# A hybrid decoder layer on one core: diagonal masking moved from TensorE to GpSimd, some loads moved to the GpSimd queue, and the FFN's first weight pieces given an earlier place in memory

## The chip, the cores and the metric

The kernel runs on one core of one Trainium2 chip. The core has five engines that run their own instruction queues: TensorE (PE, with its weight loads shown as PEld), VectorE (DVE), ScalarE (ACT), GpSimd (POOL) and SyncE (SP), which here only issues DMA transfers. ACT issues some transfers too (ACTq in the trace). The metric is the device time of one launch in microseconds. The kernel before took 2703.38 us, the median of 3 runs (2702.57 to 2706.26).

## The reference

One decoder layer over 2048 positions of width 1024, in float32:

```python
a = rms_norm(h, pre_mix_g);  z = a @ w_in          # q | k | v | f | u_sg | v_sg
logits = q @ k.T / 8 + c[t] - c[s]                 # c = cumsum(log_sigmoid(f + f_bias)); 8 heads x 64
logits = where(s <= t, logits, -inf)               # causal
y_att = softmax(logits) @ v
y_sg = gelu(u) * (tril(w_s) @ layer_norm(gelu(v)) + b_s)
h += rms_norm(concat(rms_norm(y_att), rms_norm(y_sg)) @ w_out, post_mix_g)
h += rms_norm(relu(rms_norm(h) @ w_ff1)**2 @ w_ff2, post_ffn_g)
h += sigmoid(h @ w_g + b_g) * (p @ w_pe)
```

## The kernel before

Every large product is made of three TensorE products of rounded operands: a value is split into a piece `hi`, rounded to the type float32r, and the remainder `lo`, and `mm3` (lines 102 to 106) adds hi*hi, hi*lo and lo*hi into one PSUM bank. So each operand needs a rounding (an ACT cast, a DVE copy or a POOL `tensor_scalar`) and a subtraction (DVE, mostly).

The stages, in the order of time in the trace:

1. 0 to 566 us: the input projection in four blocks of 512 positions (`block`), with `maxima(b)` of the previous block mixed in. `maxima` computes, for each head and block, products of q and k (line 169) of which DVE takes row maxima (lines 172, 175); the row maxima later enter the attention's bias. It loads q and k from a DRAM scratch into two buffers each, `QM` and `KM`, by transfers that the ACT queue issues (lines 159 and 165). Each `KM` load serves four products.
2. 566 to about 1124 us: the attention. `steps` is a list of 320 steps (head, block of 512 queries, tile `j` of 128 keys), first the blocks 0 and 1 of all heads (96 steps), then block 2 (96 steps), then block 3 (128 steps). In program order `scores` runs `LA = 4` steps ahead of `weigh`. `scores` makes two products into a PSUM bank of a pool of two (`pS`, lines 644 and 647); in the four diagonal tiles of each (head, block) a third product adds a matrix with -1e30 above the diagonal (line 649: `dmask_r` times an identity `ident_r`). Because `MASKB` is 4 and `b < MASKB` always holds, the branch in which GpSimd masks (line 653) never runs. Then ACT takes the exponential (line 651), ACT or, for the tiles in `HI_DVE`, DVE rounds it (lines 659, 657), and DVE subtracts (line 660). `weigh` makes three products with V (lines 672 to 674). Mixed in by rates are the rest of `maxima(2)`, all of `maxima(3)` (its eight heads with four `KM` loads each fall between 556 and 880 us), the V projection of the last block (`late_v`) and, in blocks 2 and 3, the output projection `project` of earlier blocks.
3. About 1124 to 1190 us: the output projection of the last block (`last_proj`), with `prep_first` mixed in: it loads `h`, transposes it, writes `cS`, and makes the operands `B[m][0]` and `B[m][1]` of the FFN's first product. The FFN multiplies by a seven-product scheme over 2x2 blocks; `join` and `join_now` make the seven right operands (`m` = 1 to 7).
4. From 1190 us: FFN, first product, 32 units. `left(i)` makes the rounded pieces `w1p` of seven combinations of W1 tiles (sums in `ws`, line 1170; cast line 991, subtraction line 994; a ring of three tiles), two calls ahead of `ff1(i)`, which multiplies. Unit 0 alone runs in two passes of 42 matmuls: first `k` = 0, 1 for all seven `m`, then `k` = 2, 3, whose operands `join2` and `join3` finish meanwhile. After that the second product, the gate and the output, to 2700 us.

The program is written in a framework that orders each engine's queue at build time and inserts the waits; a tile of a pool that is opened over memory of earlier pools waits until those tiles are released. In the kernel before, `w1p` comes from a pool of its own, "w1pp" (line 1134), that is opened only after the pools of stages 2 and 3 have been closed (lines 1131 to 1133). The tiles `px` (line 964) hold the transposed pieces in `prep_first` (line 1092), the raw operands of `join2` (`jraw`, line 1125) and those of `prep_next` (line 1107), which prepares the second half of the positions during the FFN.

Of the kernel before, what the change touches and what calls it, by code (L numbers as in the profile page):

```python
# [9 lines left out]
F32 = mybir.dt.float32  # L10
F32R = mybir.dt.float32r
AF = mybir.ActivationFunctionType
ALU = mybir.AluOpType
# [4 lines left out]
P = 128  # L18
# [3 lines left out]
HD = 64  # L22
# [5 lines left out]
NB = S // TB  # L28
# [6 lines left out]
def trunk(ctx, tc, x, p, w_in, f_bias, sg_ln_g, sg_ln_b, sg_w, sg_b, att_out_g, sg_out_g,  # L35
# [4 lines left out]
    def pool(stack, name, bufs=1, space=None, side="left"):  # L40
        kw = {} if space is None else {"space": space}
        return stack.enter_context(tc.tile_pool(name=name, bufs=bufs, side=side, reuse_waits="tile", **kw))

    sc, ve, po, pe, sy = nc.scalar, nc.vector, nc.gpsimd, nc.tensor, nc.sync

    x, p, out = x[0], p[0, 0], out[0]
# [28 lines left out]
    ve.memset(dmask, 0.0)  # L75
    po.affine_select(out=dmask_r, in_=dmask, pattern=[[-1, P]], compare_op=ALU.is_ge, fill=NEG,
                     base=0, channel_multiplier=1)
    ident_r = const1.tile([P, P], F32R, name="ident_r")
    ve.tensor_copy(ident_r, ident)

    def bcast(pool, name, v, n):
        t = pool.tile([P, n], F32, name=name)
# [59 lines left out]
    def maxima(b):  # L142

        def rows(h, mh):
            ps = place_m()
            pe.transpose(ps[:8, :P], mh.rearrange("p a b -> p (a b)").bitcast(F32), ident)
            mr = msm.tile([8, P], F32, name="mr", bufs=1)
            sc.copy(mr, ps[:8, :P])
            for l in range(2):
                sy.dma_start(qS[b, h, P + l].rearrange("(t i) -> t i", i=P), mr[4 * l:4 * l + 4])  # L150

        last = None
        ps = place_m()
        pe.matmul(ps[:, :H], ident[:, 0:1].broadcast_to([P, P]), c_all[:, 4 * b], start=True, stop=True)
        ve.tensor_copy(c0_all[:, b], ps[:, :H])
        n = 0
        for h in range(H):
            q = QM[h % 2]
            sc.dma_start(q[:HD].bitcast(F32), qS[b, h, :HD])
            mx = msm.tile([P, 4, 6], F32, name="mx")  # L160
            po.memset(mx, NEG)
            for c in range(b + 1):
                km = KM[n % NKM]
                n += 1
                sc.dma_start(km[:HD + 2].bitcast(F32), kS[c, h, HD:])
                for tt in range(4):
                    w = TB if c < b else P * (tt + 1)
                    ps = place_m()
                    pe.matmul(ps[:, :w], q[:, tt * P:(tt + 1) * P], km[:, :w], start=True, stop=True)  # L169
                    full = w if c < b else w - P  # L170
                    if full:
                        ve.tensor_reduce(mx[:, tt, c:c + 1], ps[:, :full], AX.X, ALU.max)  # L172
                    if c == b:
                        dg = ps[:, w - P:w]
                        ve.tensor_tensor_reduce(out=dg, in0=dg, in1=dmask, scale=1.0, scalar=NEG,
                                                op0=ALU.add, op1=ALU.max, accum_out=mx[:, tt, 5:6])
                    yield
            if last is not None:
                rows(*last)
            m = msm.tile([P, 4], F32, name="m")  # L180
            ve.tensor_reduce(m, mx, AX.X, ALU.max)
            ve.tensor_scalar(m, m, -1.0, c0_all[:, b, h:h + 1], ALU.mult, ALU.subtract)
            mh = msm.tile([P, 2, 4], F32R, name="mh")
            ve.tensor_copy(mh[:, 0], m)
            ve.tensor_tensor(mh[:, 1], m, mh[:, 0].bitcast(F32), ALU.subtract)
            last = (h, mh)
            yield
        yield
        rows(*last)
# [357 lines left out]
    KA = acs.tile([P, KCOLS], F32R, name="KA")  # L547
# [85 lines left out]
    outs = {}  # L633

    HI_DVE = ((), (), (1,), (1, 4, 7, 10))

    def scores(k, j):
        b, h = heads[k]
        k0 = slot(k)
        e = qset(k)  # L640
        off = max(0, j - 4 * b) * P
        js = slice(k0 + j * P, k0 + (j + 1) * P)
        ps = pS.tile([P, 512], F32, name="pS")
        pe.matmul(ps[:, off:], KS[:, js], QS[e][:, off:], start=True, stop=False)
        diag = j >= 4 * b
        by_pe = diag and b < MASKB
        pe.matmul(ps[:, off:], KA[:, js], QB[e][:, off:], start=False, stop=not by_pe)  # L647
        if by_pe:
            pe.matmul(ps[:, off:off + P], dmask_r, ident_r, start=False, stop=True)
        pr = pp.tile([P, TB], F32, name="pr")  # L650
        sc.activation(pr[:, off:], ps[:, off:], AF.Exp, bias=bias_of(b)[:, j, h:h + 1])  # L651
        if diag and not by_pe:
            po.affine_select(out=pr[:, off:off + P], in_=pr[:, off:off + P], pattern=[[1, P]],
                             compare_op=ALU.is_ge, fill=0.0, base=0, channel_multiplier=-1)
        hl = pp.tile([P, 2, TB], F32R, name="hl")
        if j % 12 in HI_DVE[b]:
            ve.tensor_copy(hl[:, 0, off:], pr[:, off:])
        else:
            sc.copy(hl[:, 0, off:], pr[:, off:])  # L659
        ve.tensor_tensor(hl[:, 1, off:], pr[:, off:], hl[:, 0, off:].bitcast(F32), ALU.subtract)  # L660
        return hl
# [148 lines left out]
                yield  # L810

    YSQ, YNO = 8, 13
    MASKB = 4
    PREPT = 54
    GAP = 2
    FIN = (0, 2)
# [144 lines left out]
    ng_pf = fsm.tile([P, KC], F32, name="ng_pf")  # L961
    ve.tensor_scalar(ng_pf, g_pf, -1.0, None, ALU.mult)
    ws = [fsm.tile([P, 4, P], F32, name=f"ws{e}") for e in range(2)]
    px = [w1q.tile([P, 4, P], F32, name=f"px{e}") for e in range(3)]

    def w1_places(pl):

        all = pl.tile([P, 3, KC, P], F32, name="w1raw")
        return all, [all[:, e] for e in range(3)]

    def w1_pieces(pl):
        return [pl.tile([P, 2, 4, P], F32R, name=f"w1p{e}") for e in range(3)]

    _, w1raw = w1_places(w1q)

# [100 lines left out]
                done(2)  # L1078
            yield

    flat = [t.rearrange("p a b -> p (a b)") for t in px]

    def prep_first():
        pa = w1raw[0].rearrange("p k f -> p (k f)")
# [12 lines left out]
    def prep_next():  # L1097

        for k in (3, 2, 1, 0):
            def place(m):  # L1100
                return Bn[m][0 if m in LATE else k % 2]

            def done(m):
                if k > 1 or k and m in LATE:
                    sy.dma_start(jS[m - 1, k - 1], place(m).bitcast(F32))

            yield from join_now(k, 1, place, done, flat[0], flat[1], px[2], px[2])

    raws, nraw, nleft = {}, 2, 0
    lefts = {}  # L1110

# [10 lines left out]
    for n, _ in enumerate(last_proj):  # L1122
        pfill.tick()
    pfill.drain()
    jraw = [flat[e] for e in range(3)] + [w1raw[1].rearrange("p k f -> p (k f)")[:, :512]]
    join_load(2, jraw)
    pl = []
    join2 = join(2, lambda: pl.pop(0), jraw)
# [2 lines left out]
    ph.close()  # L1131
    pmph.close()
    mix_stack.close()
    w1p = w1_pieces(pool(w1s, "w1pp", side="right"))

    fl = ExitStack()
    ctb = pool(fl, "ctb")
# [225 lines left out]
    for i, (u, n, ks) in enumerate(run):  # L1363
        if i == len(JR):
            for _ in jrest:
                pass
            jts.close()
            ctc = pool(fl, "ctc")
            hqp = pool(fl, "hqp")
            for t in ((0, 0), (0, 1), (1, 0), (1, 1), 5, 6):  # L1370
                hq[t] = hqp.tile([P, 512], F32, name="hq" + str(t).strip("()").replace(", ", "_"))
            for k in range(2):
                for m in range(1, 8):
                    if not (k and m in LATE):
                        Bn[m][k] = ctc.tile([P, 2, 512], F32R, name=f"C{m}_{k}")
        if i == first_of[NF - 1]:
            fill.drain()
        if i == hold:
            w1s.close()
            fr.close()  # L1380
            fr = ExitStack()
            w1q = pool(fr, "w1r", side="right")
            lrp = pool(fr, "lrp", side="right")
            lrq = pool(fr, "lrq", side="right")
            chain.append(lrp.tile([P, 4, 512], F32, name="T_0"))
            LR += [lrp.tile([P, 512], F32, name=f"lr{e}") for e in range(4)]
            w1all, w1raw = w1_places(w1q)
            w1p = w1_pieces(w1q)
            LT += [lrq.tile([P, 2, 512], F32R, name=f"L{e}") for e in range(3)]
            RT += [lrq.tile([P, 2, 512], F32R, name=f"R{e}") for e in range(3)]  # L1390
        while nl < len(run) and nl <= i + 2 and not (i < hold <= nl):
            left(nl)
            nl += 1
        ff1(i, B if u < NF else Bn)
        if u == NF - 1:
            for m, k in NEXT[n]:
                sy.dma_start(B[m][k].bitcast(F32), jS[m - 1, k - 1])
        if i < len(JR):
            for _ in range(JR[i]):
                next(jrest, None)  # L1400
        if u > 0:
            fill.tick()
        if i == first_of[NU - 2]:
            for e in range(4):
                load2(e)
        if i >= first_of[NU - 1] + 2 and len(ops2) < 3:
            combos(len(ops2))
# [214 lines left out]
```

## Time and profile before

| | |
|---|---|
| median of 3 runs | 2703.38 us |
| the profiled execution | 2701.87 us, of which the profile's span is 2700.1 us |
| TensorE's mean granted clock in the span | 0.989 of full speed |
| TensorE busy | 2613.7 us |
| VectorE busy | 1841.5 us |
| ScalarE busy | 1342.4 us |
| GpSimd busy | 811.5 us |

A row of a group view gives line, engine, operation, what it writes and reads, the count, then busy time and the mean of one in nanoseconds, then the engine's idle time just before these instructions and what ended it. A timeline row gives start and duration in microseconds and, in brackets, the idle time before it with its releaser. A row of the stretches gives the stretch, its length, and for each engine busy time and number of instructions, then the granted clock, the DMA engines' busy share and GB/s.

### The profile page before, as it was taken

The page shows a single profiled execution, that of the slowest core. Times are in us where ns is not written, and L with a number is a line of the kernel's source. Part 1 is how long each engine was busy: PE and PEld are TensorE (multiplying, and loading weights), DVE is VectorE, ACT ScalarE, POOL GpSimd, SP SyncE. Part 2 cuts the span into 40 slices and gives each one's busy share as a digit, 9 for nine tenths or more (in the row PEclk, how much of TensorE's full clock was granted, in tenths as well). Part 3 has the DMA queues.
Part 4 walks back from the last instruction along what each step waited for, and adds up shares of the span by engine and source line. Part 5 has one row for each costly group of instructions (what it writes and reads, how often), then busy time and mean ns, then how long its engine had stood idle before and what let it go on. Part 6 is the DMA issues. An engine that isn't in the chain of part 4 may idle for free.

```text
span 2700.1 us, 37436 instructions
## 1 busy us (share of the span) xinstructions
PE 2613.7 (97%) x12316; PEld 2123.4 (79%) x12316; DVE 1841.5 (68%) x3212; ACT 1342.4 (50%) x2632; POOL 811.5 (30%) x695
## 2 busy tenths in 40 slices
PE   8999999999899999969999999999999999999999
PEld 7787978777677777757788788888888888888887
DVE  5547576866778655578888676668886596875443
ACT  6444433358777777555555554544445444453111
POOL 5444343510000000253444332325451171501211
PEclk9999999999999999989999999999999999999999
DMA  5565756598868766454665854447556654673331
GB/s 169 151 183 145 195 141 171 145 218 211 210 177 190 175 182 151 137 164 165 224 210 175 296 193 148 150 155 247 171 191 223 187 160 132 210 250 115 109 119 61
DMA packets 440611, 472.85 MB, mean 175 GB/s; under 512 B 155616, under 2 KB 269664, under 8 KB 440416
## 3 DMA queue, kind: packets, MB, share of 16 engines
q1 hardware_dynamic: 430179, 454.39, 57.0%
q10 hardware_dynamic: 10237, 16.07, 2.2%
q8 instruction: 97, 1.59, 0.3%
q14 instruction: 98, 0.80, 0.1%
HBM read 336.38 MB, written 133.96 MB: 174 GB/s over the span
## 4 chain that ended last, share of the span: by engine, by line
PE 53%; DMA 2%; DVE 1%; issue 1%; ACT 1%; POOL 0%; SPq 0%; DVEq 0%; ACTq 0%; POOLq 0%
PE pf L106 17%; PE pf L104 17%; PE pf L105 17%; PE pf L1470 1%; DMA w1raw<-in_w_ff_dram 0%; DMA px<-hS 0%; DMA cS<-px 0%; DVE w1p L994 0%; DMA B<-jS 0%; PE pf L1018 0%; DVE ws L1170 0%; DVE hq L1189 0%; DVE z L748 0%; POOL tmp L1068 0%; DMA ysT<-ysS 0%
## 5 line engine op out<-in xcount | busy, mean ns | idle before, releaser
L104 PE MATMUL pf<-B,w1p 128*128 128x512 f32 x752 | 298.3, 397 | 14.4 <-ACT w1p L991 13.6
L106 PE MATMUL pf<-B,w1p 128*128 128x512 f32 x752 | 296.1, 394 | 2.8 <-DVE w1p L994 2.7
L1197 POOL TENSOR_TENSOR hq<-hq,hq 128x512 f32<-128x512 f32 x128 | 197.0, 1550 | 335.4 <-ACT hq L1191 298.3
L105 PE MATMUL pf<-B,w1p 128*128 128x512 f32 x752 | 297.1, 395 | 0.0
L660 DVE TENSOR_TENSOR hl<-pr,hl 128x512 fp32r<-128x512 f32 (+1 forms) x320 | 191.9, 608 | 102.7 <-ACT hl L659 86.0
L100 POOL TENSOR_TENSOR wsp<-wraw,wsp 128x344 fp32r<-128x344 f32 (+1 forms) x176 | 200.1, 1154 | 192.0 <-ACT wsp L96 181.6
L651 ACT ACTIVATE pr<-pS,bias 128x512 f32<-128x512 f32 (+1 forms) x320 | 196.6, 623 | 106.1 <-PE pS L647 64.0
L172 DVE TENSOR_REDUCE mx<-pM 128x1 f32<-128x512 f32 (+3 forms) x288 | 169.8, 597 | 78.7 <-PE pM L169 78.0
L104 PEld LDWEIGHTS pf<-B,w1p 128*128 128x128 f32 x752 | 141.7, 188 | 48.9 <-ACT w1p L991 14.1
L104 PE MATMUL pacc<-wsp,wide 128*128 128x344 f32 (+1 forms) x480 | 166.7, 347 | 9.7 <-ACT ug L358 6.8
L104 PE MATMUL pf<-R,L 128*128 128x512 f32 x452 | 175.9, 389 | 0.0
L106 PE MATMUL pf<-R,L 128*128 128x512 f32 x452 | 175.8, 389 | 0.0
L105 PE MATMUL pf<-R,L 128*128 128x512 f32 x452 | 175.8, 389 | 0.0
L106 PEld LDWEIGHTS pf<-B,w1p 128*128 128x128 f32 x752 | 141.5, 188 | 37.5 <-DVE w1p L994 4.4
L105 PEld LDWEIGHTS pf<-B,w1p 128*128 128x128 f32 x752 | 141.7, 188 | 31.9
L106 PE MATMUL pacc<-wsp,wide 128*128 128x344 f32 (+1 forms) x480 | 162.7, 339 | 0.5 <-DVE wide L117 0.5
L105 PE MATMUL pacc<-wsp,wide 128*128 128x344 f32 (+1 forms) x480 | 162.4, 338 | 0.0
L659 ACT CAST hl<-pr 128x512 fp32r<-128x512 f32 (+3 forms) x272 | 146.6, 549 | 6.5 <-PE pO L674 0.8
L991 ACT CAST L<-lr 128x512 fp32r<-128x512 f32 x113 | 70.3, 622 | 149.6 <-PE pf L105 119.5
L994 DVE TENSOR_TENSOR L<-lr,L 128x512 fp32r<-128x512 f32 x113 | 96.1, 851 | 68.0 <-ACT L L991 67.7
L994 DVE TENSOR_TENSOR w1p<-ws,w1p 128x512 fp32r<-128x512 f32 (+1 forms) x136 | 117.4, 869 | 35.7 <-ACT w1p L991 33.8
L991 ACT CAST w1p<-w1raw 128x512 fp32r<-128x512 f32 (+1 forms) x123 | 73.4, 598 | 128.5 <-PE pf L105 124.2
(443 smaller groups left out, 7199.1 us busy)
## 6 DMA issues: line engine op xcount, KB each, us to landing
hidC<-hq SPq DMA_DIRECT2D x224, 256.0 KB
lr<-hidC SPq DMA_DIRECT2D x224, 256.0 KB
w1raw<-in_w_ff_dram SPq DMA_DIRECT2D x64, 512.0 KB
w1raw<-in_w_ff_dram SPq DMA_DIRECT2D x128, 256.0 KB
wraw<-in_w_in_dram SPq DMA_DIRECT2D x96, 256.0 KB
wraw<-in_w_in_dram SPq DMA_DIRECT2D x88, 172.0 KB
KM<-kS ACTq DMA_DIRECT2D x80, 132.0 KB
jS<-C SPq DMA_DIRECT2D x19, 512.0 KB
```

The source lines that it names most:

```text
L100: e.tensor_tensor(dst[:, 1], src, dst[:, 0].bitcast(F32), ALU.subtract)
L104: pe.matmul(ps, l[0], r[0], start=first, stop=False)
L105: pe.matmul(ps, l[0], r[1], start=False, stop=False)
L106: pe.matmul(ps, l[1], r[0], start=False, stop=last)
L172: ve.tensor_reduce(mx[:, tt, c:c + 1], ps[:, :full], AX.X, ALU.max)
L651: sc.activation(pr[:, off:], ps[:, off:], AF.Exp, bias=bias_of(b)[:, j, h:h + 1])
L659: sc.copy(hl[:, 0, off:], pr[:, off:])
L660: ve.tensor_tensor(hl[:, 1, off:], pr[:, off:], hl[:, 0, off:].bitcast(F32), ALU.subtract)
L991: sc.copy(dst[:, 0], src)
L994: (po if lo == "pool" else ve).tensor_tensor(dst[:, 1], src, dst[:, 0].bitcast(F32), ALU.subtract)
L1197: po.tensor_tensor(t, x, y, op)
L1470: pe.transpose(ps[:, kk], hts[t][g][:, kk * P:(kk + 1) * P], ident)
```

## The change

The mask product and the identity it needed are gone; in every diagonal tile GpSimd sets the exponentials above the diagonal to zero, after the exponential and ahead of the rounding. In block 0 the rounding of tile 1, and in block 1 those of tiles 1 and 4, are made by GpSimd instead of ACT. The loads of `maxima(3)` are issued by GpSimd's queue instead of ACT's. `w1p` is allotted in the pool `w1q`, which is opened when the attention ends; to make room, two of the three `px` tiles are the `ws` tiles, `join2` reads its raw operands into `w1raw[1]`, `v_t` and the last `px`, and `prep_next` gets two tiles `pxn` of its own in a later pool.

```diff
-    ident_r = const1.tile([P, P], F32R, name="ident_r")
-    ve.tensor_copy(ident_r, ident)
...
-            sc.dma_start(q[:HD].bitcast(F32), qS[b, h, :HD])
+            qe = po if b == NB - 1 else sc
+            qe.dma_start(q[:HD].bitcast(F32), qS[b, h, :HD])
...
-                sc.dma_start(km[:HD + 2].bitcast(F32), kS[c, h, HD:])
+                qe.dma_start(km[:HD + 2].bitcast(F32), kS[c, h, HD:])
...
     HI_DVE = ((), (), (1,), (1, 4, 7, 10))
+    HI_POOL = ((1,), (1, 4), (), ())
...
-        by_pe = diag and b < MASKB
-        pe.matmul(ps[:, off:], KA[:, js], QB[e][:, off:], start=False, stop=not by_pe)
-        if by_pe:
-            pe.matmul(ps[:, off:off + P], dmask_r, ident_r, start=False, stop=True)
+        pe.matmul(ps[:, off:], KA[:, js], QB[e][:, off:], start=False, stop=True)
         pr = pp.tile([P, TB], F32, name="pr")
         sc.activation(pr[:, off:], ps[:, off:], AF.Exp, bias=bias_of(b)[:, j, h:h + 1])
-        if diag and not by_pe:
+        if diag:
             po.affine_select(out=pr[:, off:off + P], in_=pr[:, off:off + P], pattern=[[1, P]],
                              compare_op=ALU.is_ge, fill=0.0, base=0, channel_multiplier=-1)
         hl = pp.tile([P, 2, TB], F32R, name="hl")
         if j % 12 in HI_DVE[b]:
             ve.tensor_copy(hl[:, 0, off:], pr[:, off:])
+        elif j in HI_POOL[b]:
+            po.tensor_scalar(hl[:, 0, off:], pr[:, off:], 1.0, 0.0, ALU.mult, ALU.add)
         else:
             sc.copy(hl[:, 0, off:], pr[:, off:])
...
-    px = [w1q.tile([P, 4, P], F32, name=f"px{e}") for e in range(3)]
+    px = [*ws, w1q.tile([P, 4, P], F32, name="px")]
...
     _, w1raw = w1_places(w1q)
+    w1p = w1_pieces(w1q)
...
-    flat = [t.rearrange("p a b -> p (a b)") for t in px]
...
-            yield from join_now(k, 1, place, done, flat[0], flat[1], px[2], px[2])
+            yield from join_now(k, 1, place, done, *pxn, px[2], px[2])
...
-    jraw = [flat[e] for e in range(3)] + [w1raw[1].rearrange("p k f -> p (k f)")[:, :512]]
+    w1raw1 = w1raw[1].rearrange("p k f -> p (k f)")
+    jraw = [w1raw1[:, :512], w1raw1[:, 512:], v_t, px[2].rearrange("p a b -> p (a b)")]
...
-    w1p = w1_pieces(pool(w1s, "w1pp", side="right"))
...
             hqp = pool(fl, "hqp")
+            pxn = [hqp.tile([P, 512], F32, name=f"pxn{e}") for e in range(2)]
```

More of the change, by code (lines that the diff above doesn't have):

```diff
@@ L812, in trunk @@
     YSQ, YNO = 8, 13
-    MASKB = 4
     PREPT = 54
@@ L1105, in done @@
                     sy.dma_start(jS[m - 1, k - 1], place(m).bitcast(F32))
-            yield from join_now(k, 1, place, done, flat[0], flat[1], px[2], px[2])
+            yield from join_now(k, 1, place, done, *pxn, px[2], px[2])
+    pxn = None
     raws, nraw, nleft = {}, 2, 0
```

## The prediction, as made before the change was run

> **What bounds the kernel now.** I read the page first: its head, the busy times and the forty slices.
>
> ```profile
> span 2700.1 us, 37436 instructions
> PE 2613.7 (97%) x12316; PEld 2123.4 (79%) x12316; DVE 1841.5 (68%) x3212; ACT 1342.4 (50%) x2632; POOL 811.5 (30%) x695
> PE   8999999999899999969999999999999999999999
> PEclk9999999999999999989999999999999999999999
> ```
>
> TensorE is busy nearly everywhere, so only two things shorten this program: less TensorE work, and idle TensorE time. The slices (67.5 us each) show one weak place, the nineteenth, where the clock falls too. Next, the stretches: the attention in four parts, the gap at the end of the last projection, and the first FFN unit.
>
> ```profile
> 566.00:707.00 141.00, 132.70 (x738) 101.12 (x738) 93.71 (x214) 110.18 (x228) 0.24 (x2) 0.99 0.89 217
> 707.00:735.00 28.00, 23.05 (x108) 16.98 (x107) 20.38 (x45) 17.76 (x36) 0.69 (x2) 0.88 0.77 195
> 735.00:880.00 145.00, 142.89 (x704) 108.06 (x703) 113.91 (x267) 104.33 (x205) 7.86 (x16) 1.00 0.76 186
> 880.00:1124.00 244.00, 242.90 (x1176) 181.96 (x1175) 146.19 (x299) 175.98 (x343) 15.03 (x24) 1.00 0.64 155
> 1190.40:1204.00 13.60, 0.01 (x1) 0.00 (x0) 13.16 (x19) 7.72 (x18) 7.40 (x7) 0.62 0.50 165
> 1190.40:1230.00 39.60, 25.04 (x102) 20.00 (x102) 31.73 (x53) 20.30 (x44) 18.90 (x10) 0.83 0.33 108
> ```
>
> After each length stand the busy times of PE, PEld, DVE, ACT and POOL. From 735 to 1124 us TensorE lacks 3.2 us of 389, and ACT is idle for 109. In 566 to 707 TensorE lacks 8.3 us, and ACT, with 110.2 of 141, is the second busiest; 707 to 735 holds one large hole. From 1190.4 to 1204 TensorE does nothing. GpSimd is idle through the whole attention. The groups name the gap's releaser, and the mask products:
>
> ```profile
> L104 PE MATMUL pf<-B,w1p 128*128 128x512 f32 x752 | 298.3, 397 | 14.4 <-ACT w1p L991 13.6
> L649 PE MATMUL pS<-ident_r,dmask 128*128 128x128 f32 x128 | 30.4, 238 | 0.0
> ```
>
> **1. The mask products.** 128 of them go. The 238 ns is a pipelined duration, not what one occupies; that is the distance to the next start:
>
> ```profile
> 585.06 0.22 PE L649 MATMUL pS<-ident_r,dmask 128*128 128x128 f32 x1
> 585.12 0.39 PE L672 MATMUL pO<-hl,V 128*65 128x512 f32 x1
> ...
> 715.91 0.22 PE L649 MATMUL pS<-ident_r,dmask 128*128 128x128 f32 x1
> 715.96 0.41 PE L672 MATMUL pO<-hl,V 128*65 128x512 f32 x1
> ```
>
> About 0.056 us each, so 7.2 us in all. The 64 of blocks 2 and 3 lie where TensorE sets the pace: -3.6. Of the 64 of blocks 0 and 1 I count half, -1.8, because there TensorE waits for ACT anyway (next part). **Sum -5.4**, ends -7.2 and -3.6.
>
> **2. What GpSimd takes over in `scores`.** Each diagonal tile gets a new link: exponential, mask on POOL, rounding. The trace shows the operation only in the setup, and POOL's one-input rounding elsewhere; the ACT casts that go, the wait they could shorten, and the subtraction on DVE are here (the ACT rows are of 566 to 707 alone, the wait of 566 to 735):
>
> ```profile
> L76 POOL TENSOR_SCALAR_AFFINE_SELECT dmask<-dmask 128x128 fp32r<-128x128 f32 x1 | 0.3, 295 | 0.0
> L255 POOL TENSOR_SCALAR_AFFINE_SELECT upper<-ones 128x128 f32<-128x128 f32 x1 | 0.6, 569 | 0.0
> L415 POOL TENSOR_SCALAR vn<-gv 128x512 fp32r<-128x512 f32 x16 | 11.7, 735 | 19.5 <-DVE gv L414 12.1 <-DVE zf L357 2.7 <-PE pacc L106 2.6
> ...
> L659 ACT CAST hl<-pr 128x512 fp32r<-128x512 f32 x48 | 29.0, 625 | 0.7
> L659 ACT CAST hl<-pr 128x384 fp32r<-128x384 f32 x16 | 8.3, 518 | 0.2
> ...
> PE pS L644 <- ACT pr L651: 5.0, 6, 1.7
> ...
> L660 DVE TENSOR_TENSOR hl<-pr,hl 128x512 fp32r<-128x512 f32 (+1 forms) x320 | 191.9, 608 | 102.7 <-ACT hl L659 86.0
> ```
>
> A mask delays the rounding by 0.3 us at least, and by about 1.3 us at most (0.57, one DVE subtraction of 0.61 that holds POOL up, two hand-offs). If ACT's queue puts nothing between exponential and cast, ACT stands still for that time; queued behind are the next exponential, whose end frees one of the two `pS` banks for line 644, and the next casts, for which DVE and then `weigh` wait. In blocks 2 and 3 this costs nothing: 64 times 1.3 is 83 us, ACT has 109 idle, and `weigh` trails `scores` by four steps. That cover fails only if ACT's idle time there is gone. In blocks 0 and 1, 64 masks at 0.45 (between the two rows, nearer the first) are 29 us. Against that, ACT loses 24 casts, 8 x (0.518 + 2 x 0.625) = 14.1 us, and about 3 us of transfer issues, and has 30.8 us idle. POOL's new work there, 64 x 0.3 to 0.57 and 24 x 0.74, is at most 54 of 141 us. I take **0**: ends -5.0 (the waits of TensorE for ACT all go) and +34 (the slower rival below).
>
> **3. The loads of `maxima(3)`.** 8 `QM` and 32 `KM` issues leave ACT's queue for POOL's, where they stand among POOL's clearings of `mx` and the new masks. SP's queue is not touched. The hole in 707 to 735 is one of these loads:
>
> ```profile
> 706.41 0.40 PE L169 MATMUL pM<-KM,QM 128*128 128x512 f32 x1
> ...
> 713.29 0.29 ACTq L165 DMA_DIRECT2D KM<-kS  x1
> ...
> 722.08 1.22 PE L169 MATMUL pM<-KM,QM 128*128 128x512 f32 x2 [4.84 <-DMA KM<-kS]
> ...
>   PE pM L169: 5.8, 2
> ```
>
> The buffer's last reader starts at 706.41; ACT issues the load 6.9 us later, behind its own casts, and TensorE idles 4.84 us. The clock in that stretch falls to 0.88, so 28 us x 0.12 = 3.4 us run at lost speed, of which some 2 are after the idle time: 6.8 us together. An idle POOL can issue at about 707. The last row (line 165's own view: who waited for it) says that only two waits by TensorE, 5.8 us, come from all 80 loads. What a transfer costs POOL is not in the trace: 0.29 us by ACT's issue, 1.55 us by POOL's longest common operation (line 1197 of the page's groups):
>
> ```profile
> L1197 POOL TENSOR_TENSOR hq<-hq,hq 128x512 f32<-128x512 f32 x128 | 197.0, 1550 | 335.4 <-ACT hq L1191 298.3
> ```
>
> I take 0.5, nearest to the issue row. A load also waits on POOL for its buffer, and masks queue behind it; ACT's cast waits for those, inside part 2's ends. **Sum -5**, ends -6.8 and +14 (second rival).
>
> A rule of the Trainium skill speaks against this edit: "SBUF — State Buffer", section "SBUF: two separate sides", says that a transfer issued from GpSimd has its descriptors written by GpSimd's cores, which a two-port DVE copy of fp32 locks out, and elsewhere in that section gives 620 ns alone and 3100 ns beside such a copy. By it each load that meets one lands some 2.5 us later. No row here shows it.
>
> **4. The pieces of W1.** The gap, start to end:
>
> ```profile
> 1187.72 0.75 DVE L1170 TENSOR_TENSOR ws<-ws,w1raw 128x256 f32<-128x256 f32 x2
> ...
> 1190.02 0.39 PE L106 MATMUL pW<-wide,yaT 128*128 128x512 f32 x1
> ...
> 1203.59 0.40 ACT L991 CAST w1p<-w1raw 128x256 fp32r<-128x256 f32 x1
> 1204.04 0.79 PE L104 MATMUL pf<-B,w1p 128*128 128x512 f32 x1 [13.63 <-ACT w1p L991]
> 1204.63 0.63 PE L105 MATMUL pf<-B,w1p 128*128 128x512 f32 x1
> 1205.06 0.63 PE L106 MATMUL pf<-B,w1p 128*128 128x512 f32 x1
> ...
> 1209.72 0.67 DVE L994 TENSOR_TENSOR B<-j,B 128x512 fp32r<-128x512 f32 x1
> ...
> 1222.85 0.39 PE L104 MATMUL pf<-B,w1p 128*128 128x512 f32 x1
> 1223.08 0.39 PE L105 MATMUL pf<-B,w1p 128*128 128x512 f32 x1
> ```
>
> The raw W1 tiles have landed and the `ws` sums exist by 1188.5, but the cast comes at 1203.59: its destination lies in memory that the closed pools release. With `w1p` in `w1q`, free since the attention, the first three pieces can stand before 1190. TensorE then goes on at 1190.3. Before, unit 0 took 8 matmuls at 0.43 us (half clock) and 76 at 0.23: 3.4 + 17.5 = 20.9 us, to 1224.9. After, 84 x 0.23 = 19.3 us, to 1209.6: at most -15.3 us. What is late next is the second pass's last operand, which DVE finishes at 1209.72 + 0.67; six matmuls (1.4 us) follow, so 1211.8: -13.1. DVE is busy 13.16 of the gap's 13.6 us, and the pieces' subtractions now fall into it; but three of them and the sums come earlier. **Sum -12**, ends -15.3 and -6.4 (first rival). The following units are TensorE-bound, so the gain reaches the end.
>
> **5. At nothing.** The dropped cast of `ident_r` lies in the setup. That `px` shares the `ws` tiles, `jraw` moves and `pxn` comes later only reorders use of buffers: the last transposed pieces leave them before the sums' rows above. If that cover fails, the sums come later and part 4 shrinks by as much.
>
> **Sum**: -5.4 + 0 - 5 - 12 = -22.4, so the profiled execution of 2701.87 us (span 2700.1 plus 1.8 around it) becomes 2679.5. The median shown is 1.5 us above that execution: **2681 us**. With the good ends, -7.2 - 5.0 - 6.8 - 15.3 = -34.3, the median would be 2669.
>
> **The rivals.**
>
> *The joins set the pace (19%).* If DVE serves the ten extra subtractions ahead of the joins (10 x 0.35 us), the last operand comes near 1214 and unit 0 ends near 1215.4; TensorE's waits then bring the half clock back for about 3 us: 1218.5, a gain of 6.4. Total -16.8: 2687. For it: DVE is full in the gap. Against it: DVE had room before 1190.
>
> *The gap's first wait is another (9%): the change doesn't do what it says.* TensorE may still wait at 1190, for a free PSUM bank or the second W1 tile, for 10 of the 13.6 us. Part 4 gives 2 us: 2691. The sums' row at 1187.72 speaks against it.
>
> *GpSimd's loads come late (9%).* From 735 to 880 us some 20 `KM` loads alternate between two buffers, one per 7.3 us. If the wait at 722 stays and seven of them make TensorE wait 2 us, part 3 is +14 instead of -5: 2700. For it: nothing in the trace bounds a POOL transfer. Against it: only two of 80 loads are late now. The Trainium skill's rule quoted in part 3 would work in this way.
>
> *The masks stop ACT in blocks 0 and 1 (8%): slower.* There 8 of every 12 tiles are diagonal. At s us of unhidden wait per mask the stretch grows by 64 s - 17 - 30.8. At 1.28 that is 34 us; the 1.8 of part 1 and the 5 of part 3 then vanish too, since TensorE waits there in any case: 2681 + 34 + 1.8 + 5, so 2722. The kernel becomes slower than before from about s = 1.1 us, where 64 s - 47.8 reaches the 22.4 of the sum. For it: ACT already holds TensorE up there. Against it: both mask rows are under 0.6 us.
>
> **How the numbers follow.** Forecast 55%. About 0.2%, 5.4 us, is what a measurement of this kernel can tell from no change. Forecast, first and second rival are faster by more: 0.83. The late loads are within it: 0.09. The stopped ACT is slower: 0.08. The range runs from the good ends, 2668, to 2700, and leaves out the slower rival, half of the late loads, and a little below.
>
> **What would show it.** Part 1: line 649 gone, TensorE's busy time 566 to 1124 less by what 128 slots make. Part 2: the idle time before `pS` line 644 by ACT stays near 5 us; ACT's idle time before the casts, put down to POOL, is the new item. Part 3: no 4.8 us wait at line 169. Part 4: no 13.6 us before line 104, small waits for `B` instead, no half clock near 1195, unit 0 over some 20 us after the last `pW` product. Wrong would make it: POOL behind in blocks 0 and 1, waits for `KM`, or a first FFN product that starts late for another reason.

## The result, and the profile after the change

The changed kernel took 2689.91 us, the median of 5 runs (2689.4 to 2694.87), against 2703.38 us of the kernel before, also 5 runs (2701.2 to 2706.26): a ratio of 0.9944 (95% interval 0.9928 to 0.9960). Run again later beside other kernels it gave 2691.85 against 2706.12 us, 0.9953 (0.9941 to 0.9966). So the change is worth 13 to 15 us, faster, but its median lies 9 us above the 2681 forecast. One run of those below (5954 us, of the kernel with masks and early pieces) is left out of its ratio.

The profiled execution is the longest of the first five: 2694.87 us, span 2693.2. Its span is 6.9 us under that of before, half of what the medians differ by. The page of the changed kernel, its head, the busy times and two rows of slices:

```profile
span 2693.2 us, 37430 instructions
PE 2617.4 (97%) x12188; PEld 2116.3 (79%) x12188; DVE 1843.1 (68%) x3211; ACT 1326.1 (49%) x2608; POOL 890.9 (33%) x887
PE   8999999999999999989999999999999999999999
PEclk9999999999999999989999999999999999999999
```

GpSimd has 79 us more (811.5 before), ScalarE 16 us less, and the weak slice is still the nineteenth, only less so. The same stretches as in the prediction, of the changed kernel:

```profile
566.00:707.00 141.00, 132.22 (x666) 93.82 (x665) 95.00 (x216) 91.45 (x190) 43.21 (x102) 0.98 0.87 208
707.00:735.00 28.00, 26.01 (x123) 17.41 (x123) 24.50 (x50) 25.25 (x51) 5.80 (x12) 1.00 0.91 227
735.00:880.00 145.00, 140.12 (x666) 104.66 (x665) 110.80 (x259) 100.81 (x202) 28.95 (x63) 0.99 0.80 190
880.00:1124.00 244.00, 243.09 (x1153) 180.76 (x1152) 150.36 (x304) 176.37 (x345) 32.58 (x63) 1.00 0.66 158
1190.40:1204.00 13.60, 10.79 (x39) 8.14 (x39) 12.63 (x22) 8.22 (x21) 8.14 (x6) 0.85 0.37 117
1190.40:1230.00 39.60, 35.43 (x136) 27.09 (x136) 34.38 (x52) 20.52 (x43) 15.21 (x10) 0.91 0.38 119
```

From 1190.4 to 1204 TensorE is now busy 10.8 of 13.6 us, and it was 0.01. In the attention (the first four rows) its busy time is what it was, 541.4 against 541.5 us, though 128 products are gone. The mean granted clock from 566 to 1124 us is 0.99 in both kernels, so it is not the clock that stretches what is left; what does was not found. Two marks in time show where the 6.9 us come from. The last value product starts at 1123.6 us in both kernels: **the attention gains nothing**. The first sum of the second FFN unit is copied out at 1228.66 us before and 1220.69 after: the whole gain of the trace is at the boundary, 8.0 us, and 7 of them reach the end.

The groups of the changed kernel that are new or have a new releaser:

```profile
L650 POOL TENSOR_SCALAR_AFFINE_SELECT pr<-pr 128x128 f32<-128x128 f32 x128 | 49.0, 386 | 155.3 <-ACT pr L648 153.1 <-PE pS L646 1.3 <-DMA V<-vS 0.8
L164 POOL DMA_DIRECT2D KM<-kS x32 | 18.3, 571 | 93.5 <-PE pM L168 78.2 <-PE pM L144 9.2 <-PE pO L673 2.7
...
L658 ACT CAST hl<-pr 128x512 fp32r<-128x512 f32 (+3 forms) x248 | 133.6, 545 | 42.2 <-POOL pr L650 37.3 <-PE pS L646 0.7 <-PE pS L644 0.6
```

A mask takes 0.39 us in the mean, a load's issue on GpSimd 0.57, and ACT now stands 37.3 us ahead of casts that wait for masks. And the place of the old gap, TensorE's timeline:

```profile
1189.55 0.39 PE L104 MATMUL pW<-wide,yaT 128*128 128x512 f32 x1
1189.78 0.39 PE L103 MATMUL pf<-B,w1p 128*128 128x512 f32 x1
...
1197.04 0.40 PE L102 MATMUL pf<-B,w1p 128*128 128x512 f32 x1
1200.11 0.79 PE L103 MATMUL pf<-B,w1p 128*128 128x512 f32 x1 [2.67 <-DVE B L993]
1201.04 0.79 PE L104 MATMUL pf<-B,w1p 128*128 128x512 f32 x1
```

The FFN follows the projection without a break. Then the second pass waits 2.67 us for an operand of the joins, and the matmuls behind it start 0.43 to 0.93 us apart instead of 0.23.

### The profile page after: what moved, and what is told of

The parts are those of the page before. It is cut to its first block, busy times and chain, and to the rows that moved or that the text cites. A ratio compares the mean times of both kernels' runs of the same rounds, so it can differ in the third digit from the quotient of the medians.

```text
span 2693.2 us, 37430 instructions
## 1 busy us (share of the span) xinstructions
PE 2617.4 (97%) x12188; PEld 2116.3 (79%) x12188; DVE 1843.1 (68%) x3211; ACT 1326.1 (49%) x2608; POOL 890.9 (33%) x887
## 4 chain that ended last, share of the span: by engine, by line
PE 52%; DVE 2%; DMA 2%; issue 1%; POOL 0%; ACT 0%; SPq 0%; DVEq 0%; POOLq 0%; ACTq 0%
PE pf L104 17%; PE pf L102 17%; PE pf L103 17%; DMA w1raw<-in_w_ff_dram 1%; DVE w1p L993 1%; DVE ws L1169 1%; PE pf L1470 1%; PE pf L1017 0%; DMA B<-jS 0%; DMA ysT<-ysS 0%; DMA ws<-hS 0%; DVE B L993 0%; DVE hq L1188 0%; DMA px<-hS 0%; POOL tmp L1067 0%
## 5 line engine op out<-in xcount | busy, mean ns | idle before, releaser
L658 ACT CAST hl<-pr 128x512 fp32r<-128x512 f32 (+3 forms) x248 | 133.6, 545 | 42.2 <-POOL pr L650 37.3
L993 DVE TENSOR_TENSOR w1p<-ws,w1p 128x512 fp32r<-128x512 f32 (+1 forms) x136 | 120.0, 886 | 31.1 <-ACT w1p L990 29.5
L168 PE MATMUL pM<-KM,QM 128*128 128x512 f32 (+2 forms) x320 | 121.2, 383 | 16.8 <-DVE mx L171 7.7
```

The source lines that it names most:

```text
L993: (po if lo == "pool" else ve).tensor_tensor(dst[:, 1], src, dst[:, 0].bitcast(F32), ALU.subtract)
```

## The experiments

Two theories to begin with. **A**: the masks on GpSimd give back inside the attention what they save, and the loads on GpSimd's queue make up for it; the gain is the gap's. **B**: the masks pay and the loads cost. **C** goes with either: at the boundary the joins on VectorE set the pace.

### The parts one by one

W1's pieces alone (masks, roundings and loads as before); masks and roundings alone; the change without its loads; the change without its masks and roundings. The edits are those of the diff above, undone by part; as an example, the loads:

```diff
-            qe = po if b == NB - 1 else sc
-            qe.dma_start(q[:HD].bitcast(F32), qS[b, h, :HD])
+            sc.dma_start(q[:HD].bitcast(F32), qS[b, h, :HD])
```

W1's pieces alone:

> Only the allotment of W1's rounded pieces is changed; masks by TensorE, all loads on ACT's queue. Theory A (the masks and the loads cancel each other inside the attention, and the whole gain is the gap's): the same time as the changed kernel, about 2690 us, 13 under before; the attention ends where it did before, the gap of 13.6 us goes, and 8 of the 13 us are left after unit 0. Theory B (the gap is worth only what is left after unit 0, 7 to 8 us, and masks plus loads give the other 6): about 2695.5 us. By the term of the prediction (12 us): 2691.5.

Masks and roundings alone:

> Only the masks of blocks 0 and 1 .. 3 move from TensorE to GpSimd, with the three roundings on GpSimd; loads on ACT's queue, W1's pieces late. Theory A (ACT's casts wait for the masks; masks cost, loads pay): about 2708 us, 5 over before, with some 35 us of idle time of ACT ahead of its casts put down to POOL, and the 4.8 us wait for KM near 722 us still there. Theory B (the masks pay what the prediction's first term says, the loads cost): 2698 us, 5.4 under before. No effect of either: 2703.

Masks, roundings and W1's pieces, without the loads:

> The changed kernel with the loads of the last maxima back on ACT's queue: masks on GpSimd and the early pieces of W1. Theory A (the loads are worth 5 us): 2695, 5 over the changed kernel, the 4.8 us wait for KM near 722 us comes back. Theory B (the loads on GpSimd cost 5): 2685. Neither: 2690.

Loads and W1's pieces, without the masks and roundings:

> The changed kernel with the masks back on TensorE (128 products) and without the roundings on GpSimd: loads on GpSimd's queue and the early pieces of W1. Theory A (masks cost 5, loads pay 5): 2685, and the wait for KM near 722 us is gone. Theory B (masks pay 5.4, loads cost): 2695, with new waits of TensorE for KM. Neither: 2690.

Measured, with all that follows, against the kernel before on the same chip. "Attention" is the time from the start of the first exponential to that of the last value product; "boundary" is that from the last projection product to the copy of the second unit's first sum, both by the timeline of the one profiled execution; "KM waits" are TensorE's from 566 to 1124 us, with their number.

| kernel | masks | last KM loads | ratio (95%) | attention | KM waits | boundary |
|---|---|---|---|---|---|---|
| before | TensorE | ACT | 1 | 554.2 | 5.8, 2 | 38.6 |
| before, second profile | TensorE | ACT | | 558.5 | 6.9, 3 | 38.7 |
| masks alone | POOL | ACT | 1.0016 (1.0006 to 1.0026) | 566.2 | 14.6, 4 | 39.5 |
| W1's pieces alone | TensorE | ACT | 0.9946 (0.9934 to 0.9959) | 553.2 | 3.8, 2 | 30.1 |
| loads + pieces | TensorE | POOL | 0.9938 (0.9923 to 0.9953) | 554.9 | 2.2, 1 | 30.1 |
| masks + pieces | POOL | ACT | 0.9972 (0.9961 to 0.9983) | 559.2 | 9.6, 4 | 30.1 |
| the change | POOL | POOL | 0.9944 (0.9928 to 0.9960) | 553.2 | 5.8, 3 | 31.1 |
| the change, second profile | POOL | POOL | 0.9953 (0.9941 to 0.9966) | 554.9 | 8.0, 4 | 30.1 |
| masks of blocks 2, 3 only | both | POOL | 0.9937 (0.9920 to 0.9954) | 550.0 | 3.2, 1 | 30.6 |
| without POOL's roundings | POOL | POOL | 0.9954 (0.9937 to 0.9970) | 550.7 | 3.3, 2 | 31.0 |
| masks + pieces, three KM | POOL | ACT | 0.9934 (0.9915 to 0.9953) | 549.4 | 1.6, 1 | 30.1 |
| joins on VectorE | POOL | POOL | 0.9948 (0.9930 to 0.9965) | 554.5 | 4.7, 2 | 27.4 |
| three KM, joins on VectorE | POOL | ACT | 0.9941 (0.9926 to 0.9956) | 550.7 | 1.8, 1 | 27.5 |
| blocks 2, 3, joins on VectorE | both | POOL | 0.9934 (0.9919 to 0.9948) | 550.9 | 4.7, 3 | 27.4 |

The two profiles of one kernel differ by 1.7 and 4.3 us in the attention, and masks alone and masks + pieces, whose attention code is the same, by 7.0. So a difference there of less than some 7 us is by itself no more than a hint; the boundary repeats within 1.1 us.

- **W1's pieces alone give the ratio of the whole change** (2691.21 against 2705.73 us, 14.5 us). Masks and loads together are worth nothing that can be measured. The boundary falls from 38.6 to 30 us in every kernel that has them.
- **Masks on GpSimd cost** where the loads stay with ACT: by the ratios 4.3 us alone (3.3 by the medians) and 7 us beside the early pieces, with intervals that don't meet. That is theory A; B (2698 us for the masks alone) is out.
- The loads make that good: 0.9972 becomes 0.9944 or 0.9953. With the masks on TensorE they change 0.9946 to 0.9938, which is within the intervals. That the loads are worth 5 us by themselves, as A has it, is not borne out: the median there is 2692.3 us, where A gave 2685 and B 2695. Nor does the wait near 722 us come back with the loads on ACT: in masks + pieces the four KM waits stand at 698, 735, 866 and 889 us.

### How the masks cost: the waits for KM

TensorE's waits named KM as the thing that grew. In the kernel with masks and early pieces, loads on ACT's queue, the timeline has this (the first row is the last reader of a KM buffer, the second the load that refills it, the third that load's first reader):

```profile
706.75 0.63 PE L167 MATMUL pM<-KM,QM 128*128 128x512 f32 x1
...
728.04 0.29 ACTq L163 DMA_DIRECT2D KM<-kS  x1
...
734.67 0.73 PE L167 MATMUL pM<-KM,QM 128*128 128x512 f32 x2 [1.88 <-DMA KM<-kS]
```

The buffer is free after 707.4, but ACT's queue comes to the load 20.7 us later. Over the 30 refills of the last maxima the longest time from the start of the last reader to the issue is 21.3 us here, 7.3 us before the change, and 2.0 us in the changed kernel, where GpSimd issues. What keeps ACT from the load is work, not waiting. The stretch between the two moments (busy times of PE, PEld, DVE, ACT and POOL, then the granted clock):

```profile
707.40:728.04 20.64, 20.43 (x92) 13.36 (x92) 18.55 (x34) 20.11 (x40) 4.14 (x8) 0.96 0.68 179
```

ACT is busy for 20.1 of 20.6 us, and 0.2 us of the rest is a wait for a mask. The load stands far back in the order of ACT's queue, which is fixed at build time: 16 exponentials of score tiles that come after the buffer's last reader in TensorE's order are ahead of it (as many with the masks alone), where before the change never more than 5 were. So moving masks and roundings changed this order too.

Lateness is not all of it. The load above costs TensorE 1.88 us, another one, issued 8.7 us after its buffer's last reader, 1.78. The other two of the four waits, 5.9 of 9.6 us, follow loads that were issued within 0.8 us. The longest of them:

```profile
878.67 0.39 PE L167 MATMUL pM<-KM,QM 128*128 128x512 f32 x1
...
879.09 0.29 ACTq L163 DMA_DIRECT2D KM<-kS  x1
...
889.39 0.47 PE L167 MATMUL pM<-KM,QM 128*128 128x512 f32 x1 [3.74 <-DMA KM<-kS]
```

Here 10.3 us pass between issue and first read. And behind three of the four waits TensorE runs at half clock (granted 0.50 from 698.9 to 709.2, 866.2 to 869.6 and 890.1 to 893.5 us), which adds to their price. A third buffer lets each load go one use earlier, whichever of the two makes it late. If these waits are what the masks cost, a third buffer on the same ACT queue should take the cost away:

```diff
-    NKM = 2
+    NKM = 3
...
-            m = msm.tile([P, 4], F32, name="m")
-            ve.tensor_reduce(m, mx, AX.X, ALU.max)
+            m = mx[:, :, 5]
+            ve.tensor_reduce(m, mx[:, :, :5], AX.X, ALU.max)
```

> Masks on GpSimd and early pieces of W1, loads of the last maxima on ACT's queue as before, but three buffers for KM instead of two, so that a load can be issued one use earlier (the row maxima's result moves into a free column of mx to make room). Theory A (with the masks on GpSimd, ACT's queue issues these loads late, and TensorE waits 9.6 us for KM; that is why masks cost 7 us without the change of queue): the KM waits of 9.6 us fall under 3, and the time falls to that of the changed kernel, ratio 0.994. Rival (the masks cost by themselves, through ACT's casts): the waits for KM go but the ratio stays near 0.997.

It does. The waits of TensorE for KM (microseconds in total, number, longest), first in the kernel with two buffers, then with three, where ACT's wait for the masks stands below:

```profile
PE pM L167 <- DMA KM<-kS: 9.6, 4, 3.7
```

```profile
PE pM L167 <- DMA KM<-kS: 1.6, 1, 1.6
...
ACT hl L657 <- POOL pr L649: 35.4, 71, 1.7
```

The attention falls from 559.2 to 549.4 us and the ratio from 0.9972 to 0.9934, and the intervals don't meet. ACT still waits 35.4 us for masks there (34.0 with two buffers), so these waits by themselves cost TensorE next to nothing; the cost goes by way of the KM buffers. How much of it is the place of the loads in ACT's queue (one is still issued 21.2 us after its buffer's last reader, and the wait of 1.6 us is for it) and how much the time from issue to first read was not taken apart. Nor was a third buffer run with the masks on TensorE, or the moved row maximum `m` without a third buffer, so what each of these two is worth by itself is not known.

### Blocks 0 and 1, and the roundings

Masks on GpSimd for blocks 2 and 3 only:

```diff
+        by_pe = diag and b < MASKB
+        pe.matmul(ps[:, off:], KA[:, js], QB[e][:, off:], start=False, stop=not by_pe)
+        if by_pe:
+            pe.matmul(ps[:, off:off + P], dmask_r, ident_r, start=False, stop=True)
...
-        if diag:
+        if diag and not by_pe:
...
-    HI_POOL = ((1,), (1, 4), (), ())
+    HI_POOL = ((), (), (), ())
...
+    MASKB = 2
```

> The changed kernel with the masks of blocks 0 and 1 back on TensorE (64 products) and no rounding on GpSimd; masks of blocks 2 and 3, the loads and W1's pieces as in the change. Theory A (a mask on GpSimd pays its 0.056 us of TensorE in blocks 2 and 3, where ACT has room, and costs in blocks 0 and 1, where ACT's cast waits for it): 3 to 4 us under the kernel with all masks on TensorE, the attention about 551 us from the first exponential on (554.9 there, 553.3 in the changed kernel); ratio to before near 0.992. Rival (masks on GpSimd give back everywhere what they save): ratio 0.994, attention near 554.

The change without the three roundings (only the `HI_POOL` line):

> The changed kernel without the three roundings per head that GpSimd took over in blocks 0 and 1; ACT casts those 24 tiles again. If the roundings relieve ACT there (the prediction's reading), ACT's busy time in 566 to 707 rises by some 14 us and the attention grows by 2 us or more. If what costs in blocks 0 and 1 is the chain exponential, GpSimd, next engine, it stays the same or shrinks by up to 3 us, and ACT's waits for masks stay near 13 us in that stretch.

Both attentions are shorter than the change's (550.0 and 550.7 against 553.2 and 554.9), and neither total is told from it (0.9937 and 0.9954 against 0.9944 and 0.9953). Without the roundings ACT has 8 us more in the first stretch:

```profile
566.00:707.00 141.00, 130.43 (x665) 91.44 (x664) 92.73 (x217) 99.60 (x209) 27.46 (x80) 1.00 0.88 209
```

So the roundings relieve ACT, by 99.6 minus 91.5 us, and TensorE has nothing from it: the attention does not grow by the 2 us that the prediction's reading asked for. ACT's waits for masks fall there from 12.7 to 8.6 us, where GpSimd no longer has roundings to make. That blocks 0 and 1 lose some 3 us by what GpSimd does in them (553.2 against 550.0), and blocks 2 and 3 gain some 5 (550.0 against the 554.9 of loads + pieces), is a hint of single profiles; whether masks or roundings do it stays open.

### The joins at the boundary

In the changed kernel, VectorE and GpSimd just before the wait for B:

```profile
1193.86 2.99 POOL L1045 TENSOR_TENSOR j<-r,r 128x512 f32<-128x512 f32 x2
1193.92 3.48 DVE L744 SCALAR_TENSOR_TENSOR z<-z,zr,g_post 128x512 f32<-128x512 f32 x2 [0.44 <-POOL zr L741]
...
1196.81 1.49 POOL L1012 TENSOR_TENSOR px<-px,hr_all 128x512 f32<-128x512 f32 x1
1197.32 2.13 DVE L747 TENSOR_TENSOR z<-z,xt 128x512 f32<-128x512 f32 x2
...
1199.37 1.28 DVE L993 TENSOR_TENSOR B<-r,B 128x512 fp32r<-128x512 f32 x2
```

Two instructions of line 744 take 3.48 us together. The line's own view, of the same kernel, gives least, median and longest of its 32:

```profile
L744 DVE SCALAR_TENSOR_TENSOR z<-z,zr,g_post x32: 737/750/1778, 759.7 to 1195.6; 128x512 f32<-128x512 f32 x32
```
The long ones here lie beside GpSimd's two-input instructions, end to end: the join's two subtractions and, for line 747, the multiplication of line 1012. The subtraction for B stands behind them in VectorE's queue. Moving the join's two GpSimd subtractions to VectorE:

```diff
-        for m, t, x, y, e in ((5, t1, rb, ra, po), (6, t2, rd, t1, ve), (7, t3, rd, rb, po), (4, t4, t2, rc, ve)):
+        for m, t, x, y, e in ((5, t1, rb, ra, ve), (6, t2, rd, t1, ve), (7, t3, rd, rb, ve), (4, t4, t2, rc, ve)):
```

> The changed kernel with two of the four subtractions of each early join moved from GpSimd to VectorE. Theory C (in the gap VectorE's instructions stretch from 0.7 to 1.74 us while GpSimd's two-input subtraction runs, so the joins set the second pass): the four z instructions from 1193.9 on fall back to about 0.7 us, the wait of 2.67 us for B shrinks to under 1.5, the half clock behind it goes, and the first FFN unit ends 2 to 4 us earlier. Rival (VectorE is simply full there): two more subtractions of 0.68 us on it, the wait for B stays or grows by 1 us.

The same lines of VectorE in that kernel:

```profile
1193.92 1.76 DVE L744 SCALAR_TENSOR_TENSOR z<-z,zr,g_post 128x512 f32<-128x512 f32 x2 [0.44 <-POOL zr L741]
1195.60 1.28 DVE L747 TENSOR_TENSOR z<-z,xt 128x512 f32<-128x512 f32 x2
1196.81 1.28 DVE L993 TENSOR_TENSOR B<-r,B 128x512 fp32r<-128x512 f32 x2
```

Four instructions that took 5.6 us take 3.0, though VectorE has more to do (the multiplication of line 1012 now comes later too, at 1199.59 us), and the operand's subtraction starts 2.6 us earlier. TensorE's waits from 1190.4 to 1230 us in that kernel:

```profile
PE pf L104 <- DVE w1p L993: 2.9, 3, 1.9
PE pf L102 <- ACT w1p L990: 1.1, 2, 0.8
```

No wait for B is left; W1's pieces come last now. The granted clock in that stretch is 1.00 (0.91 in the change), and the boundary takes 27.4 us where it took 31.1 and 30.1. That is theory C with its mechanism. It holds in the three kernels that have the edit, but 3 us of 2690 are not told apart in the totals.

### Both edits, and both kernels again

Three KM buffers and joins on VectorE:

> Two edits together: loads of the last maxima on ACT's queue with three KM buffers, and the early joins' subtractions on VectorE; masks on GpSimd and early pieces of W1 as in the change. If the two gains lie in different places (attention: 3.8 us against the changed kernel; first FFN unit: 3.8 us) they add: about 7 us under the changed kernel on the same chip, ratio to before near 0.992. If the second is lost later, as a gain at the boundary can be, ratio 0.9935.

Masks of blocks 2 and 3, and joins on VectorE:

> Masks of blocks 2 and 3 alone on GpSimd, loads on GpSimd's queue with two buffers, early joins' subtractions on VectorE. By the traces: 3.2 us less attention than the changed kernel and 3.8 us less first unit, about 7 us under it, ratio near 0.992; without the second gain 0.9935.

The changed kernel again:

> The changed kernel once more, to have it beside the two above on one chip, and a second profile of it (its first profile was the longest of its five runs). If the small losses after the first unit (8.8 us ahead after unit 2, 6.8 after unit 8) belong to one execution, the second profile ends 8 to 9 us before the profiled run of before; if they belong to the kernel, 7.

The kernel before again:

> The kernel before once more, for a second profile. If the 4.84 us wait for KM at 722 us is a fixture of it, it is there again (the prediction's third term leaned on it); if it belongs to one execution, as the kernel with W1's pieces alone suggests, which runs the same attention with waits for KM of 1.2 and 2.5 us, the wait is shorter or elsewhere.

On one chip: 2689.35, 2687.36 and 2691.85 us, against 2706.12 of before. The attention and the boundary are shorter as expected, and the three buffers with joins on VectorE have the shortest span of all profiles (2683.1 us, 10.1 under the change's first), but the medians stand 2.5 and 4.5 us under the change's, with intervals that overlap. **No version is shown to beat the change.** The second profile of the change has a span of 2692.1 us, 8.0 under the first one of the kernel before, between the 7 and the 8 to 9 of the two readings; the two profiles of before differ by 3.1 us themselves, so whose the small loss after the first unit was stays open. The second profile of the kernel before has the wait for KM again:

```profile
723.03 1.22 PE L169 MATMUL pM<-KM,QM 128*128 128x512 f32 x2 [4.34 <-DMA KM<-kS]
```

So the wait at 722 us is in both profiles of the kernel before. But W1's pieces alone, with the same attention code, have less at that place:

```profile
720.38 0.72 PE L170 MATMUL pM<-KM,QM 128*128 128x512 f32 x2 [1.25 <-DMA KM<-kS]
```

There the load is issued as late as before, 6.9 us after its buffer's last reader starts, but it is read 5.2 us after its issue, where 8.8 and 8.3 us passed in the two profiles of before. So late issue alone does not make this wait; why the load came sooner was not found. Nor is it known why medians differ by 13 to 14 us and these spans by 7 to 11: the profiled executions of the change lie 5.0 and 2.0 us above its medians and those of the kernel before 1.5 and 1.2 us below, and nothing in the traces says what a longer run lost.

## Why the prediction was right, and where it was wrong

Right: the sign, the range, and that the gap is most of it. Wrong: 9 us too much, in the terms of the attention, which measure at about nothing where -10.4 was counted.

1. **Mask products, -5.4.** TensorE did get 128 products fewer, and GpSimd's mask takes what the rows said, 0.39 us in the mean (between 0.3 and 0.57). With a third buffer the attention is 3.8 to 9 us shorter than in the kernels with all masks on TensorE (549.4 against 553.2 to 558.5), which fits the saving, but none of those has a third buffer, so the saving is not shown by itself. In the change as made it does not reach the end.
2. **The work in `scores` at 0: this step failed where the loads stay with ACT.** I asked whether the next exponential and the casts behind a waiting cast have time to spare; they do, as the 35 us of waits in the three-buffer kernel show. I did not ask about the loads of `maxima(3)`, and these have none: alone, masks cost 4.3 us instead of saving 5.4, and beside the early pieces 7, and a third KM buffer takes that away. ACT's standing still is not what makes the latest load late (0.5 us of idle time ahead of it), its place in the queue is; and more than half of the waiting is for loads that were not late. The slower rival (stopped ACT, 2722) was about this engine and these blocks, but its price, 34 us of TensorE's waits for ACT, is not what happened: those waits at line 644, from 566 to 735 us, fell from 5.0 to 1.2 us.
3. **Loads on GpSimd, -5: this step failed in the change itself.** The wait of 4.84 us is gone, the issue costs 0.57 us, as taken (0.5), and no load is issued more than 2.0 us after its buffer's last reader starts. But TensorE waits as long for KM in sum as before, 5.8 and 8.0 us in the two profiles against 5.8 and 6.9: the loads that it waits for are first read 4.6 to 9.7 us after their issue. The term put the wait down to the late issue alone, 6.9 us, and not to the 8.8 us from issue to first read in the same rows. The gain is not one of its own either. With masks on TensorE it is -2 within the error; with masks on GpSimd it is 5 to 8, the price of step 2. So terms 1 to 3, -10.4 in sum, are about 0. Late loads, the third rival in the list (part 3 calls it the second), came in small: three and four waits of 1.2 to 2.6 us. The line's own view of the changed kernel (nanoseconds of an issue, then microseconds from issue to landing):

```profile
L164 POOL DMA_DIRECT2D KM<-kS x32: 525/573/749, 571.2 to 883.2; - x32
...
DMA to landing us min/median/max: 2.5/4.8/9.1
```

The rule of the Trainium skill that spoke against this edit ("SBUF — State Buffer", section "SBUF: two separate sides") is not decided here. No issue takes over 0.75 us. Six of the 32 loads have a VectorE rounding by copy (line 654) beginning within 2 us after their own start and land after 5.5 to 9.1 us, the other 26 after 2.5 to 8.5. But the load at one of the six places (854.79 us) was first read 7.9 us after its issue before the change too, when ACT issued it. So how much of the 4.8 us is the queue's stays open.
4. **W1's pieces, -12.** 14.5 us by the medians when made alone, 12 by the ratios when made on top of the masks (1.0016 to 0.9972), 7.5 to 9.4 at the boundary by the traces. By the medians the term was about right, by the traces the gain is a fifth to over a third smaller, so that the term fits is in part luck. Its path was the first rival's: the joins' operand came last, 2.67 us late, with the half clock behind it, and the rival's price was 6.4. Its cause was in the timeline of before, and I did not read it there:

```profile
1195.09 3.42 DVE L745 SCALAR_TENSOR_TENSOR z<-z,zr,g_post 128x512 f32<-128x512 f32 x2 [0.44 <-POOL zr L742]
```

I counted VectorE as full where it was being held.
5. **At nothing**: no wait for `px`, `pxn` or the moved raw operands is among TensorE's at the boundary. It held.

The hold has a rule. The Trainium skill, "SBUF — State Buffer", section "SBUF: two separate sides", says that VectorE and GpSimd share a pair of ports as an exclusive lock, which a VectorE instruction with two SBUF inputs takes against a GpSimd instruction that reads SBUF; whoever comes first holds it to the end. The trace agrees: two instructions of 0.75 us each take 3.48 us beside subtractions of 1.5, and 1.76 when those are taken away.

## What to carry to other kernels

When an edit moves work between engines, look up where the transfer issues come to stand in their queues, how long after the release of its buffer each one goes out, and how long it then takes until its result is read; one buffer more can be worth as much as another queue. When a kernel has gains in several places, measure each part alone and each left out: here two of three terms were each other's price. Before calling an engine full, compare the duration of its instructions with the median of their line: a stretched one names the engine beside it.

## What the runs showed of the hardware that was not expected

- A two-input VectorE instruction of 128x512 takes up to 1.78 us beside GpSimd's two-input subtractions (1.5 us each), with 0.75 in the median of its line. Moving GpSimd's two subtractions onto the busy VectorE shortened VectorE's chain by 2.6 us.
- GpSimd's issue of a 132 KB load takes 0.57 us of its time, where ACT's queue shows 0.29.
- After the wait of 2.67 us at the boundary TensorE ran at half clock for 6.8 us in the change's first profile and for 3.4 us in its second and with W1's pieces alone, behind the same wait.
- Loads of 132 KB that were issued within 0.8 us after their buffer's last reader started were first read, by a waiting TensorE, up to 10.3 us (ACT's queue, masks and pieces) and 9.7 us (GpSimd's queue, the change) after their issue.
